# Expert weights of a mixture-of-experts stage laid out by pair of experts and by transfer

## Chip, cores and metric

The kernel runs on one core of one Trainium2 chip. The metric is the device time of one launch in microseconds. Laying out the inputs on the host is not part of it.

## The reference

The reference is two transformer blocks over 256 tokens of 1024 features, in float32. Block 1 is a mixer (gated long convolution, short convolution, pooling), a cross attention and a mixture of 32 experts, of which each token takes 4. Block 2 has attention, retention and feed-forward layers. The change touches the experts only:

```
def clamped_swiglu(gu):
    gate = jnp.minimum(gu[..., :D_EXPERT], SWIGLU_LIMIT)
    up = jnp.clip(gu[..., D_EXPERT:], -SWIGLU_LIMIT, SWIGLU_LIMIT)
    return (up + 1.0) * (gate * jax.nn.sigmoid(gate * SWIGLU_ALPHA))
...
    def step(acc, blk):
        tok, g, e = blk
        xb = h_pad[tok]
        act = clamped_swiglu(xb @ w_gu[e] + b_gu[e])
        yb = act @ w_down[e] + b_down[e]
        return acc.at[tok].add(yb * g[:, None].astype(yb.dtype)), None
```

`w_gu` is 32 x 1024 x 2048 and `w_down` 32 x 1024 x 1024, together 402.7 MB of float32. That is most of the 650.58 MB that the kernel moves.

## The kernel before

Everything is unrolled, on one core. The order on each engine is set by the Tile scheduler, from the order of the code and from a few `issue_after` constraints.

**The experts go in 16 pairs**, numbered 0 to 15 here. A pair's two experts share the array: each has up to 64 token columns (CAP), expert 2i on rows 0 to 63 of the result and expert 2i+1 on rows 64 to 127. For a pair the program does, in order:

- `gather` (L1703): the tokens' rows by one-hot products, done a pair ahead, in two halves;
- `gate_up` (L1716): 8 steps of k, each with 4 banks and 2 experts, every step reading one 2 MB tile `wgu`;
- `swiglu` (L1752 to L1756): the activation, begun by the DVE instruction of L1752 when the first bank of step 7 is done;
- `turn` (L1763, L1764): transposes;
- the down products (L1874): four blocks (j, h), each reading one 2 MB tile `wdn`;
- `combine` (L1770, L1771): the weighted sums go back to the tokens, one pair late.

**The weights** are streamed by SyncE's queue (SP). A pair is 8 tiles `wgu` and 4 tiles `wdn`, 12 x 2 MB = 25.17 MB. Nine buffers of 2 MB take them in turn (five of the pool `raw`, four of a pool `pre`; a tenth is used once). SP issues the transfers in program order, and each waits until the matmuls on the tile nine places earlier are done. The addresses, in `load`:

```
r["g", k] = raw([128, 2, 2 * D], "wgu")
nc.sync.dma_start(r["g", k], A["wgu"][e, 128 * k:128 * k + 128].rearrange("x p n -> p x n"))
...
r["d", j, h] = raw([128, 2, 4, 512], "wdn")
```

In DRAM a row of `wgu` is 8 KB, so a partition's 16 KB of a tile come in two runs of 8 KB, one for each expert. A partition's 16 KB of a `wdn` tile come in eight runs of 2 KB, in two transfers of 1 MB. The other weights (`wpre`, `wpost`, `wadb`; tiles `wraw`, `wadb`) are packed on the host already, and a partition's 16 KB lie together there.

**A branch** (L1855) stands in pair 3: if an expert has more than 64 tokens, `overflow` runs. It is not taken with these inputs. SP waits at the branch until the transfers that it has issued have landed.

After pair 15 come the sums for the norm (`stats`, L1076), the first products of block 2 (`begin`, L399 to L401), and the norm of x3 (L1224 and on).

Of the kernel before, what the change touches and what calls it, by code (L numbers as in the profile page):

```python
# [11 lines left out]
F32 = mybir.dt.float32  # L12
# [51 lines left out]
# ---------------------------------------------------------------- host layout  # L64
# [15 lines left out]
def _slices(w, cols):  # L80
    """[K, 256 columns] -> one [128, 256] slice per 128 rows."""
    b = w[:, cols]
    return [b[k * 128:(k + 1) * 128] for k in range(b.shape[0] // 128)]


def _pack(slices):
    """slices of [128, 256], eight to a block, two blocks to a transfer."""
    n = len(slices)
    while len(slices) % 16:
        slices.append(slices[-1])  # L90
    a = np.stack(slices).reshape(-1, 16, 128, 256)
    return np.ascontiguousarray(a.transpose(0, 2, 1, 3)), n
# [6 lines left out]
def _moba_cols():  # L99
    """columns of a q or k projection: heads 8-15 as chunks of four heads' halves."""  # L100
    idx = list(range(512))
    for g in range(2):
        for half in range(2):
            for h in range(4):
                base = (8 + 4 * g + h) * 64 + half * 32
                idx += list(range(base, base + 32))
    return np.array(idx)


def host_layout(inp):  # L110
# [87 lines left out]
    r["wgu"] = A["w_gu"][0]  # L198
    r["wdn"] = A["w_down"][0]
# [3 lines left out]
    # constants of the shapes alone  # L203
    k = np.arange(128)
    later = -(k[:, None] > k[None, :]).astype(np.float32)       # minus later rows
    earlier = (k[:, None] < k[None, :]).astype(np.float32)      # earlier rows
    io = np.broadcast_to(np.arange(128, dtype=np.float32), (128, 128))
    r["cst4"] = np.ascontiguousarray(np.concatenate([earlier, io], axis=1))
    cst = [np.eye(128, dtype=np.float32)]                       # identity
# [19 lines left out]
    caus = np.where(k[:, None] >= q[None, :], 0.0, NEG)      # [query, key]  # L229
    strict = (k[:, None] < q[None, :])                        # [key, query]  # L230
# [16 lines left out]
# ---------------------------------------------------------------- the program  # L247


class Weights:  # L250
    """A stream of weight slices [128, 256], split into two float32r parts."""
# [23 lines left out]
    def split(self, eng=None):  # L275
        """the next GR slices"""
# [37 lines left out]
def program(ctx: ExitStack, tc: tile.TileContext, A, out, stop=None):  # L314
# [17 lines left out]
    # ---- inputs and constants that stay  # L332
# [53 lines left out]
    class Part:  # L386
        """a product of a block of weights, in parts"""
# [45 lines left out]
    def product_tok(st, XH, XL, kcs, evac, taps=0):  # L433
        """out [128 tokens, 256 features] for both token tiles."""
# [17 lines left out]
    def broad(pool, tag):  # L452
        """two parts of a product's operand with room for columns past the tokens"""
# [23 lines left out]
    def behind(*ins):  # L477
        """what follows queues behind these on their engines"""
# [83 lines left out]
    def normal(src, dst, H, L, c, nm, g, b, func=None):  # L562
        """dst = (src - mean) / deviation * g + b for chunk c, or its two parts"""
# [28 lines left out]
    # ---- modulation vectors of block 2, computed where the array would wait  # L592
# [6 lines left out]
    def silu_c(pool, after=None):  # L599
        """silu of the condition on all partitions"""  # L600
# [7 lines left out]
    def vector_ada(n=1):  # L608
        """modulation vectors by rows, a chunk of 128 to an instruction"""
# [33 lines left out]
    def norm_constants():  # L643
        """weights of the sums which the norm of x3 = (a - mean) / dev * g + b takes from a"""
# [13 lines left out]
    def router_constants():  # L658
        """router weights by gain and a column for the mean; the sums its norm's mean and shift bring"""
# [81 lines left out]
        # ---- pooling windows  # L741
# [23 lines left out]
        # ---- short gated convolution  # L765
# [46 lines left out]
        # ---- memory norm (its own sums, off the main chain)  # L812
# [33 lines left out]
        # ---- keys and values of the memory, spread over the waits of the norms  # L846
# [25 lines left out]
        # ---- norm of the long convolution, and its output  # L872
# [22 lines left out]
        # ---- mix, first norm  # L895
# [24 lines left out]
        # ---- cross attention  # L920
# [76 lines left out]
        # ---- output, and on the way the tokens' rows, their sums and the router's products  # L997
# [56 lines left out]
    # ---- sums over features of the experts' output, tokens on the partitions  # L1054
# [25 lines left out]
    def begin(n):  # L1080
        """the first block of block 2's products, before its input is normalised"""
# [9 lines left out]
    # ======================================================== block 1: experts  # L1091
# [9 lines left out]
    # ======================================================== block 2  # L1101
    wst = post_w
    wst.aside = ASIDE
    with tc.tile_pool(name="wp2", bufs=3, reuse_waits="tile") as wp, tc.tile_pool(name="post", bufs=1, reuse_waits="tile") as post:
# [8 lines left out]
        def project_h(evac, taps=0, into=None):  # L1113
            """a block of the products of the normalised input, the first ones before it is scaled"""
# [110 lines left out]
        # ---- x3 = (a - mean) rs g + b and h = x3 rm gs + shift from sums of a alone  # L1225
# [98 lines left out]
        # ---- layer 0: heads 0-7 by stick-breaking, 8-15 by softmax over their block  # L1324
        with tc.tile_pool(name="att", bufs=1, reuse_waits="tile") as at:
# [123 lines left out]
            def schedule(first, second, half):  # L1449
                """the heads' stages, each a step behind the one before it"""  # L1450
# [33 lines left out]
        # ---- layer 1: retention  # L1484
# [92 lines left out]
def experts(tc, A, B, pre, mo, tmp, psum, X0, consts, Stat, normal, col, eps5, L, x2t, nmu, sd, bgu, es_ins, stats, spread, norm_constants, begin):  # L1577
# [24 lines left out]
    def load(i):  # L1602
# [3 lines left out]
        e = slice(2 * i, 2 * i + 2)  # L1606
        for k in range(NCH):
            r["g", k] = raw([128, 2, 2 * D], "wgu")
            nc.sync.dma_start(r["g", k], A["wgu"][e, 128 * k:128 * k + 128].rearrange("x p n -> p x n"))
        for j in range(2):  # L1610
            for h in range(2):
                r["d", j, h] = raw([128, 2, 4, 512], "wdn")
                if 2 * i + h < 2 * WD or not j:
                    for x in range(2):
                        nc.sync.dma_start(r["d", j, h][:, x], A["wdn"][2 * i + x, 512 * h:512 * h + 512, 512 * j:512 * j + 512].rearrange("(k p) n -> p k n", p=128))
                else:
                    for k in range(4):
                        o = 512 * h + 128 * k
                        nc.sync.dma_start(r["d", j, h][:, :, k], A["wdn"][e, o:o + 128, 512 * j:512 * j + 512].rearrange("x p n -> p x n"))
# [6 lines left out]
    def biased(i, banks, js=range(4)):  # L1626
        """the sums of experts 2i and 2i + 1, begun with their biases"""
# [11 lines left out]
    # ---- router  # L1639
# [25 lines left out]
    # ---- places: how many earlier tokens took the expert  # L1665
# [20 lines left out]
    # ---- one-hot rows, gathering  # L1686
    def gather(i, then=None):
        """the tokens of experts 2i and 2i + 1, CAP columns each; their weighted places"""
# [39 lines left out]
    def residual():  # L1728
        """the norm's output"""
# [46 lines left out]
    def overflow(work):  # L1776
        """Tokens past the first CAP of an expert, any number of them."""
        with tc.For_i(0, NE, 1) as e:
            pc, gc = tmp((128, 2, 1), tag="mx"), tmp((128, 2, 1), tag="sm")
            V.tensor_copy(pc, posm[:, :, bass.ds(e, 1)])  # L1780
            V.tensor_copy(gc, gates[:, :, bass.ds(e, 1)])
            bt = work.tile([4, 512], F32, tag="bo", name="bo")
            nc.sync.dma_start(bt, A["bgu"].rearrange("(e j) n -> e j n", j=4)[bass.ds(e, 1)].rearrange("e j n -> (e j) n"))
            xo = mo.tile([128, D], F32, tag="xs", name="xo")
            act = work.tile([128, D], F32, tag="Y", name="acto")
            at = work.tile([128, D], F32, tag="actT", name="ato")
            actT = at.rearrange("p (k s) -> p k s", k=NCH)

            def piece(src):
                w = tmp((128, 512), tag="pd", bufs=2)  # L1790
                nc.sync.dma_start(w, src.rearrange("e p n -> (e p) n"))
                return w

            for r in range(2):
                pr = tmp((128, 2, 1), tag="mx")
                V.tensor_scalar(pr, pc, float(-(CAP + 128 * r)), None, op0=ALU.add)
                So, Go = tmp((128, 2, 128)), tmp((128, 2, 128))
                for t in range(2):
                    V.tensor_scalar(So[:, t, :], iota, pr[:, t, :], None, op0=ALU.is_equal)
                    V.tensor_scalar(Go[:, t, :], So[:, t, :], gc[:, t, :], None, op0=ALU.mult)  # L1800
                for k in range(NCH):
                    p = psum([128, 128], tag="tp", bufs=2)
                    for t in range(2):
                        PE.matmul(p, x2t[:, t, k * 128:k * 128 + 128], So[:, t, :], start=(t == 0), stop=(t == 1))
                    S.activation(xo[:, k * 128:k * 128 + 128], p, AF.Identity, scale=col("ln2_g", k), bias=col("ln2_b", k))
                gst = psum([128, T], tag="tp", bufs=2)
                for t in range(2):
# [97 lines left out]
```

## Time and profile before

| what | value |
|---|---|
| median of 3 runs | 2246.17 us (2244.93 to 2249.36) |
| span of the profiled execution | 2244.0 us, 2.2 us under that median |
| PE busy | 2103.7 us, 94% |
| DVE, ACT, POOL busy | 54%, 36%, 24% |
| moved by the DMA engines | 650.58 MB, mean 290 GB/s |
| granted clock of TensorE, mean | 0.979 |

Times of the trace count from the span's start. "GB/s" is what the 16 DMA engines moved in a stretch. "DMA share" is the time that their packets took as a share of 16 engines' time; packets overlap a little, so that it can go over 1. The experts' transfers run from about 430 to 1450 us.

### The profile page before, as it was taken

How to read it: one execution, taken by the hardware profiler on the slowest of the kernel's cores; microseconds unless marked ns; L12 is line 12 of the kernel's file. 1: busy time of each engine (PE TensorE's matmuls, PEld its weight loads, DVE VectorE, ACT ScalarE, POOL GpSimd, SP SyncE). 2: the span in 40 equal slices, each digit the busy share in tenths (PEclk: the TensorE clock that was granted, in tenths of full speed). 3: DMA queues.
4: the chain of work that ended last, by engine and by line, in shares of the span. 5: the costliest groups of instructions: out<-in, count | busy, mean ns of one | idle time of the engine just before them, and what ended most of it. 6: DMA issues, size and time to landing. Idle time of an engine off the chain costs nothing.

```text
span 2244.0 us, 33058 instructions
## 1 busy us (share of the span) xinstructions
PE 2103.7 (94%) x13668; PEld 1523.0 (68%) x13668; DVE 1202.3 (54%) x1807; ACT 797.2 (36%) x1374; POOL 544.9 (24%) x452
## 2 busy tenths in 40 slices
PE   8989979999999999999999999889999999999998
PEld 8889978873443333333333333378799999999998
DVE  7999988942222222221112222278788679777554
ACT  5556566641000000000000000157475565556443
POOL 2756396512000000000000000076422124220001
PEclk9999989999999999999999999989999999999999
DMA  8344445589999999999999999954366557555540
GB/s 353 148 155 151 155 186 225 216 338 391 404 414 384 399 408 407 408 409 410 411 411 409 407 408 407 408 195 180 151 260 268 223 195 269 227 224 216 198 151 20
DMA packets 123548, 650.58 MB, mean 290 GB/s; under 512 B 6624, under 2 KB 8544, under 8 KB 76160
## 3 DMA queue, kind: packets, MB, share of 16 engines
q1 hardware_dynamic: 122048, 645.46, 73.1%
q10 hardware_dynamic: 1344, 2.95, 0.4%
q8 instruction: 109, 1.79, 0.3%
q14 instruction: 47, 0.39, 0.0%
HBM read 647.33 MB, written 1.05 MB: 289 GB/s over the span
## 4 chain that ended last, share of the span: by engine, by line
PE 42%; DMA 13%; DVE 8%; ACT 2%; issue 2%; POOL 1%; SPq 1%; DVEq 0%; ACTq 0%; POOLq 0%
DMA wgu<-in_wgu 12%; PE ps_st L1874 9%; PE ps_mm L417 7%; PE ps_mm L419 7%; PE ps_mm L418 7%; PE ps_mm L1716 4%; DVE wl L289 2%; PE ps_tp L1770 2%; DVE act L1756 1%; PE ps_mm L1632 1%; PE ps_tp L1703 1%; POOL tmp_pd L1755 1%; ACT wh L288 1%; DMA wdn<-in_wdn 1%; PE ps_mm L443 1%
## 5 line engine op out<-in xcount | busy, mean ns | idle before, releaser
L289 DVE TENSOR_TENSOR wl<-wraw,wh 128x1024 fp32r<-128x1024 f32 x352 | 500.4, 1426 | 179.7 <-ACT wh L288 175.5
L1716 PE MATMUL ps_mm<-wgu,xs 128*64 128x512 f32 x2048 | 457.2, 595 | 30.9 <-DMA wgu<-in_wgu 30.4
L288 ACT ACTIVATE wh<-wraw 128x1024 fp32r<-128x1024 f32 x356 | 374.4, 1054 | 243.6 <-PE ps_mm L418 218.4
L1716 PEld LDWEIGHTS ps_mm<-wgu,xs 128*64 128x64 f32 x2048 | 144.2, 137 | 315.5 <-issue 256.3
L1752 DVE TENSOR_SCALAR tmp_pd<-ps_mm 128x512 f32<-128x512 f32 x32 | 22.0, 692 | 416.8 <-PE ps_mm L1716 416.8
L1874 PE MATMUL ps_st<-wdn,actT 128*64 128x512 f32 x1024 | 239.9, 597 | 5.7 <-DVE actT L1764 5.6
L417 PE MATMUL ps_mm<-HH,wh 128*128 128x256 f32 x832 | 236.8, 286 | 1.5 <-ACT wh L288 1.2
L419 PE MATMUL ps_mm<-HH,wl 128*128 128x256 f32 x832 | 234.9, 285 | 1.5 <-DVE wl L289 1.5
L418 PE MATMUL ps_mm<-HL,wh 128*128 128x256 f32 x832 | 236.3, 285 | 0.0
L1755 POOL TENSOR_TENSOR tmp_pd<-tmp_pd,tmp_stat 128x512 f32<-128x512 f32 x32 | 40.1, 1275 | 787.5 <-ACT tmp_stat L1753 737.8
L620 POOL TENSOR_TENSOR wadb<-wadb,cb 128x1024 f32<-128x1024 f32 x60 | 169.8, 2855 | 142.0 <-DMA wadb<-in_wadb 86.7
L1753 ACT ACTIVATE tmp_stat<-tmp_pd 128x512 f32<-128x512 f32 x32 | 20.2, 631 | 497.3 <-DVE tmp_pd L1752 497.3
L417 PE MATMUL ps_mm<-pairA,wh 128*128 128x256 f32 x640 | 181.7, 289 | 11.9 <-ACT wh L288 8.5
L419 PE MATMUL ps_mm<-pairA,wl 128*128 128x256 f32 x640 | 181.3, 289 | 4.7 <-DVE wl L289 4.5
L418 PE MATMUL ps_mm<-pairA,wh 128*128 128x256 f32 x640 | 182.5, 287 | 2.3 <-DVE pairA L475 2.3
L1874 PEld LDWEIGHTS ps_st<-wdn,actT 128*64 128x64 f32 x1024 | 75.3, 137 | 142.3 <-issue 132.6
L417 PEld LDWEIGHTS ps_mm<-HH,wh 128*128 128x128 f32 x832 | 159.9, 192 | 2.9 <-ACT wh L288 1.9
L419 PEld LDWEIGHTS ps_mm<-HH,wl 128*128 128x128 f32 x832 | 159.2, 192 | 2.5 <-DVE wl L289 1.9
L418 PEld LDWEIGHTS ps_mm<-HL,wh 128*128 128x128 f32 x832 | 160.1, 192 | 0.8 <-issue 0.7
L417 PEld LDWEIGHTS ps_mm<-pairA,wh 128*128 128x128 f32 x640 | 123.9, 195 | 14.0 <-ACT wh L288 9.1
L419 PEld LDWEIGHTS ps_mm<-pairA,wl 128*128 128x128 f32 x640 | 123.5, 195 | 7.0 <-DVE wl L289 7.0
L418 PEld LDWEIGHTS ps_mm<-pairA,wh 128*128 128x128 f32 x640 | 125.3, 196 | 2.7 <-DVE pairA L475 2.7
(460 smaller groups left out, 4219.1 us busy)
## 6 DMA issues: line engine op xcount, KB each, us to landing
wgu<-in_wgu SPq DMA_DIRECT2D x128, 2048.0 KB, 22.3
wdn<-in_wdn SPq DMA_DIRECT2D x124, 1024.0 KB, 14.5
wraw<-in_wpost SPq DMA_DIRECT2D x56, 2048.0 KB, 8.0
wraw<-in_wpre SPq DMA_DIRECT2D x32, 2048.0 KB, 7.7
wadb<-in_wadb SPq DMA_DIRECT2D x24, 2048.0 KB, 8.9
wdn<-in_wdn SPq DMA_DIRECT2D x8, 512.0 KB, 12.2
wraw<-in_wpre SPq DMA_DIRECT2D x4, 512.0 KB, 7.7
wraw<-in_wpost SPq DMA_DIRECT2D x4, 512.0 KB, 11.8
```

Of the source, the lines that this page charges most:

```text
L288: self.ins = (nc.scalar.activation(wh, src, AF.Copy).ins, (eng or nc.vector).tensor_tensor(wl, src, wh.bitcast(F32), op=ALU.subtract).ins)
L289: (eng or nc.vector).tensor_tensor(wl, src, wh.bitcast(F32), op=ALU.subtract).ins)
L417: PE.matmul(pts[m], wh[:, w], XH[:, kc, :width], start=(i == 0), stop=False)
L418: PE.matmul(pts[m], wh[:, w], XL[:, kc, :width], start=False, stop=False)
L419: PE.matmul(pts[m], wl[:, w], XH[:, kc, :width], start=False, stop=(i == n - 1))
L443: PE.matmul(pts[t], XH[:, kc, x], wl, start=False, stop=False)
L620: G.tensor_tensor(w[:, i, :], w[:, i, :], cbs[0], op=ALU.mult)
L1632: PE.matmul(banks[j][row[x]], ident[:, o:o + 1].to_broadcast([128, CAP]), bgu, start=True, stop=False)
L1716: i_ = PE.matmul(banks[j][row[x]], xs[:, k, row[x]], r["g", k][:, x, 512 * j:512 * j + 512], start=False, stop=(k == NCH - 1))
L1755: G.tensor_tensor(g, g, s, op=ALU.mult)
L1770: PE.matmul(p[:, m, :], Y[:, (2 * c + m) * 128:(2 * c + m) * 128 + 128], GST, start=True, stop=True)
L1874: PE.matmul(yb[j][row[x]], actT[:, k, row[x]], r["d", j, k // 4][:, x, k % 4, :], start=(k == 0), stop=(k == NCH - 1))
```

## The change

Two arrays are laid out on the host in the order of the transfers. `wgu` gets the shape [pair, k, partition, expert, column], and `wdn` [pair, j, h, partition, k, expert, column]. Each 2 MB transfer now reads one block of DRAM in which a partition's 16 KB lie together. A `wdn` tile is one transfer where it was two; the last two tiles of pair 15 are still four transfers of 512 KB each. Inside the tile `wdn` the places of expert and k are exchanged, and the matmuls' slice with them.

`overflow` becomes a loop over pairs with a loop over the two experts inside, since its addresses now need both numbers. Comments are gone too, and line numbers move by one to three.

```diff
-    r["wgu"] = A["w_gu"][0]
-    r["wdn"] = A["w_down"][0]
+    r["wgu"] = np.ascontiguousarray(A["w_gu"][0].reshape(NE // 2, 2, NCH, 128, 2 * D).transpose(0, 2, 3, 1, 4))
+    r["wdn"] = np.ascontiguousarray(A["w_down"][0].reshape(NE // 2, 2, 2, 4, 128, 2, 512).transpose(0, 5, 2, 4, 3, 1, 6))
...
-        e = slice(2 * i, 2 * i + 2)
         for k in range(NCH):
             r["g", k] = raw([128, 2, 2 * D], "wgu")
-            nc.sync.dma_start(r["g", k], A["wgu"][e, 128 * k:128 * k + 128].rearrange("x p n -> p x n"))
+            nc.sync.dma_start(r["g", k], A["wgu"][i, k])
         for j in range(2):
             for h in range(2):
-                r["d", j, h] = raw([128, 2, 4, 512], "wdn")
+                r["d", j, h] = raw([128, 4, 2, 512], "wdn")
                 if 2 * i + h < 2 * WD or not j:
-                    for x in range(2):
-                        nc.sync.dma_start(r["d", j, h][:, x], A["wdn"][2 * i + x, 512 * h:512 * h + 512, 512 * j:512 * j + 512].rearrange("(k p) n -> p k n", p=128))
+                    nc.sync.dma_start(r["d", j, h], A["wdn"][i, j, h])
                 else:
                     for k in range(4):
-                        o = 512 * h + 128 * k
-                        nc.sync.dma_start(r["d", j, h][:, :, k], A["wdn"][e, o:o + 128, 512 * j:512 * j + 512].rearrange("x p n -> p x n"))
+                        nc.sync.dma_start(r["d", j, h][:, k], A["wdn"][i, j, h, :, k])
...
-        with tc.For_i(0, NE, 1) as e:
+        with tc.For_i(0, NE // 2, 1) as e:
+            with tc.For_i(0, 2, 1) as x:
+                overflow_of(work, e, x)
...
-                    PE.matmul(yb[j][row[x]], actT[:, k, row[x]], r["d", j, k // 4][:, x, k % 4, :], start=(k == 0), stop=(k == NCH - 1))
+                    PE.matmul(yb[j][row[x]], actT[:, k, row[x]], r["d", j, k // 4][:, k % 4, x, :], start=(k == 0), stop=(k == NCH - 1))
```

The scheduler also orders a few instructions differently. On SP, the end of pair 5's transfers and the start of pair 6's, before:

```order
320 L1609 DMA wgu_7261<-in_wgu 128x2x2048
321 L1615 DMA wdn_7263<-in_wdn 128x4x512 x2
322 L1615 DMA wdn_7266<-in_wdn 128x4x512 x2
323 L1615 DMA wdn_7269<-in_wdn 128x4x512 x2
324 L1615 DMA wdn_7272<-in_wdn 128x4x512 x2
325 L1609 DMA wgu_7474<-in_wgu 128x2x2048
```

The same place in the changed kernel:

```order
325 L1609 DMA wgu_7253<-in_wgu 128x4096
326 L1614 DMA wdn_7255<-in_wdn 128x4096
327 L1614 DMA wdn_7257<-in_wdn 128x4096
328 L1614 DMA wdn_7259<-in_wdn 128x4096
329 L1614 DMA wdn_7261<-in_wdn 128x4096
330 L1609 DMA wgu_7462<-in_wgu 128x4096
```

The tiles come in the same order, and 12 transfers stand where 16 stood.

On PE, where pair 4's `combine` meets the first step of pair 5 (`ps_tp` from `Y` is `combine`, `ps_tp` from `z` is `gather`, `ps_mm` is `gate_up`), before:

```order
3640 L1770 MATMUL ps_tp_7376<-tmp_t_7193,Y_7210 128x256 x2
3641 L1770 MATMUL ps_tp_7380<-tmp_t_7193,Y_7210 128x256 x2
3642 L1703 MATMUL ps_tp_7391<-tmp_t_7384,z_5056 128x128 x8
3643 L1716 MATMUL ps_mm_7275<-wgu_7247,xs_7163 64x512 x2
3644 L1716 MATMUL ps_mm_7278<-wgu_7247,xs_7163 64x512 x2
3645 L1716 MATMUL ps_mm_7281<-wgu_7247,xs_7163 64x512 x2
3646 L1716 MATMUL ps_mm_7284<-wgu_7247,xs_7163 64x512 x2
3647 L1703 MATMUL ps_tp_7404<-tmp_t_7384,z_5056 128x128 x8
3648 L1716 MATMUL ps_mm_7275<-wgu_7249,xs_7163 64x512 x2
```

The same place in the changed kernel:

```order
3647 L1768 MATMUL ps_tp_7364<-tmp_t_7185,Y_7202 128x256 x2
3648 L1768 MATMUL ps_tp_7368<-tmp_t_7185,Y_7202 128x256 x2
3649 L1714 MATMUL ps_mm_7263<-wgu_7239,xs_7155 64x512 x2
3650 L1714 MATMUL ps_mm_7266<-wgu_7239,xs_7155 64x512 x2
3651 L1714 MATMUL ps_mm_7269<-wgu_7239,xs_7155 64x512 x2
3652 L1714 MATMUL ps_mm_7272<-wgu_7239,xs_7155 64x512 x2
3653 L1701 MATMUL ps_tp_7379<-tmp_t_7372,z_5056 128x128 x8
3654 L1701 MATMUL ps_tp_7392<-tmp_t_7372,z_5056 128x128 x8
3655 L1714 MATMUL ps_mm_7263<-wgu_7241,xs_7155 64x512 x2
```

Both halves of `gather` now stand behind step 0; before, step 0 stood between them.

On ACT, in the norm after the experts (`wh` is a part of block 2's weights, `tmp_t` from `tmp_r4` serves the norm's broadcast), before:

```order
657 L1244 ACTIVATE tmp_u_9890<-tmp_u_9890,kc_93 128x2
658 L288 ACTIVATE wh_10102<-wraw_10048 128x1024
659 L491 ACTIVATE tmp_t_9977<-cst_69,tmp_r4_9885 128x128
660 L491 ACTIVATE tmp_t_9980<-cst_69,tmp_r4_9885 128x128
661 L1253 ACTIVATE tmp_mu_9907<-ps_tp_9908 128x256
```

The same place in the changed kernel:

```order
663 L1245 ACTIVATE tmp_u_9840<-tmp_u_9840,kc_93 128x2
664 L492 ACTIVATE tmp_t_9927<-cst_69,tmp_r4_9835 128x128
665 L492 ACTIVATE tmp_t_9930<-cst_69,tmp_r4_9835 128x128
666 L289 ACTIVATE wh_10052<-wraw_9998 128x1024
667 L1254 ACTIVATE tmp_mu_9857<-ps_tp_9858 128x256
```

The weights' part `wh` moved behind the two `tmp_t`.

## Rows read from the trace of the kernel before

**Rows 1.** The page: the span in 40 equal slices.

```profile
PE   8989979999999999999999999889999999999998
DMA  8344445589999999999999999954366557555540
```

**Rows 2.** The page: DMA packets, and issues (count, KB each, us to landing).

```profile
DMA packets 123548, 650.58 MB, mean 290 GB/s; under 512 B 6624, under 2 KB 8544, under 8 KB 76160
...
wgu<-in_wgu SPq DMA_DIRECT2D x128, 2048.0 KB, 22.3
wdn<-in_wdn SPq DMA_DIRECT2D x124, 1024.0 KB, 14.5
```

**Rows 3.** The chain, pairs 5 to 15: start, us, what (L1752 begins a pair's activation).

```profile
821.18 0.70 DVE tmp_pd L1752
...
878.65 0.70 DVE tmp_pd L1752
...
936.12 0.70 DVE tmp_pd L1752
...
1022.71 33.81 DMA wgu<-in_wgu
...
1057.68 0.70 DVE tmp_pd L1752
...
1119.25 0.70 DVE tmp_pd L1752
...
1428.18 0.70 DVE tmp_pd L1752
```

**Rows 4.** Stretches: busy us of each engine (x), clock, DMA share, GB/s.

```profile
12.00:40.00 28.00, 27.58 (x226) 27.17 (x226) 21.55 (x30) 14.97 (x23) 6.72 (x7) 1.00 1.02 429
1022.00:1056.00 34.00, 30.74 (x154) 12.85 (x152) 1.80 (x3) 0.38 (x1) 0.00 (x0) 1.00 1.01 418
1057.00:1077.00 20.00, 19.11 (x88) 6.78 (x86) 9.44 (x17) 3.37 (x7) 3.27 (x4) 1.00 1.05 390
...
960.00:1430.00 470.00, 429.64 (x2008) 164.64 (x2006) 87.26 (x156) 27.98 (x63) 22.43 (x27) 1.00 1.02 409
...
560.00:720.00 160.00, 153.59 (x732) 67.34 (x729) 40.90 (x74) 11.37 (x24) 9.79 (x12) 0.99 1.02 407
...
728.70:809.10 80.40, 78.63 (x382) 33.28 (x380) 15.00 (x26) 4.11 (x9) 3.26 (x4) 1.00 1.00 401
...
240.00:260.00 20.00, 19.04 (x156) 18.43 (x155) 17.69 (x31) 10.14 (x15) 7.27 (x7) 1.00 0.56 211
```

**Rows 5.** PE around `gather` and step 0: start, us, line, tiles, count.

```profile
849.38 2.05 PE L1703 MATMUL ps_tp<-tmp_t,z 128*128 128x128 f32 x16
851.36 3.65 PE L1716 MATMUL ps_mm<-wgu,xs 128*64 128x512 f32 x16
```

**Rows 6.** Waits, 960 to 1430 us: total us, times, longest.

```profile
PE ps_mm L1716 <- DMA wgu<-in_wgu: 30.4, 27, 1.4
```

**Rows 7.** SP, the last `wgu` of pair 5: issue, and us to landing; PE's end of step 7.

```profile
L1609 SPq DMA_DIRECT2D wgu<-in_wgu x1: 367/367/367, 784.9 to 784.9; - x1
...
DMA to landing us min/median/max: 24.2/24.2/24.2
...
823.53 1.03 PE L1632 MATMUL ps_mm<-moec,cst 128*64 128x512 f32 x4
```

**Rows 8.** SP at the branch, and its last transfer before it.

```profile
L1855 SPq EVENT_SEMAPHORE  x8: 17/17/17, 723.1 to 728.5; - x8
...
L1609 SPq DMA_DIRECT2D wgu<-in_wgu x1: 368/368/368, 700.0 to 700.0; - x1
...
DMA to landing us min/median/max: 28.1/28.1/28.1
```

**Rows 9.** ACT in the norm after the experts.

```profile
1473.74 1.06 ACT L288 ACTIVATE wh<-wraw 128x1024 fp32r<-128x1024 f32 x1 [3.21 <-PE ps_mm L418]
1474.70 0.68 ACT L491 ACTIVATE tmp_t<-cst,tmp_r 128x128 f32<-128x128 f32 x2
```

More of the change, by code (lines that the diff above doesn't have):

```diff
@@ L1776, in overflow @@
     def overflow(work):
-        with tc.For_i(0, NE, 1) as e:
[L1779 to L1797, printed above, removed]
-                for t in range(2):
[L1799 to L1807, printed above, removed]
-                    PE.transpose(gst[:, t * 128:t * 128 + 128], Go[:, t, :], ident)
-                GST = tmp()
-                V.tensor_copy(GST, gst)
-                banks = [psum([128, 512]) for _ in range(4)]
-                for j in range(4):
-                    PE.matmul(banks[j], ident[0:4, j:j + 1].to_broadcast([4, 128]), bt, start=True, stop=False)
-                for k in range(NCH):
-                    for j in range(4):
-                        w = piece(A["wgu"][bass.ds(e, 1), k * 128:k * 128 + 128, 512 * j:512 * j + 512])
-                        PE.matmul(banks[j], xo[:, k * 128:k * 128 + 128], w, start=False, stop=(k == NCH - 1))
-                swiglu(banks, act)
-                turn(act, actT)
-                yb = [psum([128, 512], tag="st", bufs=2) for _ in range(2)]
-                for k in range(NCH):
-                    for j in range(2):
-                        w = piece(A["wdn"][bass.ds(e, 1), k * 128:k * 128 + 128, 512 * j:512 * j + 512])
-                        PE.matmul(yb[j], actT[:, k, :], w, start=(k == 0), stop=(k == NCH - 1))
-                for j in range(2):
-                    V.tensor_copy(act[:, 512 * j:512 * j + 512], yb[j])
-                combine(act, GST)
@@ new lines, in overflow, with overflow_of, piece @@
+        with tc.For_i(0, NE // 2, 1) as e:
+            with tc.For_i(0, 2, 1) as x:
+                overflow_of(work, e, x)
+    def overflow_of(work, e, x):
+        pc, gc = tmp((128, 2, 1), tag="mx"), tmp((128, 2, 1), tag="sm")
+        V.tensor_copy(pc, posm[:, :, bass.ds(2 * e + x, 1)])
+        V.tensor_copy(gc, gates[:, :, bass.ds(2 * e + x, 1)])
+        bt = work.tile([4, 512], F32, tag="bo", name="bo")
+        nc.sync.dma_start(bt, A["bgu"].rearrange("(e j) n -> e j n", j=4)[bass.ds(2 * e + x, 1)].rearrange("e j n -> (e j) n"))
+        xo = mo.tile([128, D], F32, tag="xs", name="xo")
+        act = work.tile([128, D], F32, tag="Y", name="acto")
+        at = work.tile([128, D], F32, tag="actT", name="ato")
+        actT = at.rearrange("p (k s) -> p k s", k=NCH)
+        def piece(src):
+            w = tmp((128, 512), tag="pd", bufs=2)
+            nc.sync.dma_start(w, src.rearrange("e p x n -> (e p) (x n)"))
+            return w
+        for r in range(2):
+            pr = tmp((128, 2, 1), tag="mx")
+            V.tensor_scalar(pr, pc, float(-(CAP + 128 * r)), None, op0=ALU.add)
+            So, Go = tmp((128, 2, 128)), tmp((128, 2, 128))
+            for t in range(2):
+                V.tensor_scalar(So[:, t, :], iota, pr[:, t, :], None, op0=ALU.is_equal)
+                V.tensor_scalar(Go[:, t, :], So[:, t, :], gc[:, t, :], None, op0=ALU.mult)
+            for k in range(NCH):
+                p = psum([128, 128], tag="tp", bufs=2)
+                for t in range(2):
+                    PE.matmul(p, x2t[:, t, k * 128:k * 128 + 128], So[:, t, :], start=(t == 0), stop=(t == 1))
+                S.activation(xo[:, k * 128:k * 128 + 128], p, AF.Identity, scale=col("ln2_g", k), bias=col("ln2_b", k))
+            gst = psum([128, T], tag="tp", bufs=2)
+            for t in range(2):
+                PE.transpose(gst[:, t * 128:t * 128 + 128], Go[:, t, :], ident)
+            GST = tmp()
+            V.tensor_copy(GST, gst)
+            banks = [psum([128, 512]) for _ in range(4)]
+            for j in range(4):
+                PE.matmul(banks[j], ident[0:4, j:j + 1].to_broadcast([4, 128]), bt, start=True, stop=False)
+            for k in range(NCH):
+                for j in range(4):
+                    w = piece(A["wgu"][bass.ds(e, 1), k, :, bass.ds(x, 1), 512 * j:512 * j + 512])
+                    PE.matmul(banks[j], xo[:, k * 128:k * 128 + 128], w, start=False, stop=(k == NCH - 1))
+            swiglu(banks, act)
+            turn(act, actT)
+            yb = [psum([128, 512], tag="st", bufs=2) for _ in range(2)]
+            for k in range(NCH):
+                for j in range(2):
+                    w = piece(A["wdn"][bass.ds(e, 1), j, k // 4, :, k % 4, bass.ds(x, 1), :])
+                    PE.matmul(yb[j], actT[:, k, :], w, start=(k == 0), stop=(k == NCH - 1))
+            for j in range(2):
+                V.tensor_copy(act[:, 512 * j:512 * j + 512], yb[j])
+            combine(act, GST)
```

## The prediction

> **What bounds the kernel now.** I read the page's slices first, then the DMA part, the chain through the experts, stretches chosen from that chain, and the waits. The page's slices [rows 1] show two kernels in one: before and after the experts, DMA is a third to two thirds busy and PE is full; through the experts (slices 9 to 25) DMA stands at 9 tenths, and PE is nearly full as well. So in this stage the two are close, and the question is which ends last, pair by pair.
>
> The chain answers it [rows 3]. The activation's first instruction (L1752) marks one moment of each pair. From pair 5 to 6 it takes 57.47 us (821.18 to 878.65), from 6 to 7 57.47 again (936.12), and between them the chain holds no transfer: that is the pace of the PE program. From pair 9 to 10 it takes 61.57 (1057.68 to 1119.25), and each pair has a piece like the 33.81 us of DMA at 1022.71: there the weights set the pace. The check: 25.17 MB over the 409 GB/s of that stretch [rows 4] is 61.5 us. The waits agree: PE stands 30.4 us in 27 gaps for a `wgu` [rows 6]. So only the time from about pair 7 on is bound by DMA; earlier pairs lived on a lead. How large the lead was: the last `wgu` of pair 5 landed at 784.9 + 24.2 = 809.1, and its step begins 16 matmuls before the row at 823.53 [rows 7]; a step takes 3.44 us (the row at 851.36, 3.65 for 16 matmuls, less the last one's tail of 0.2 [rows 5]). That is 820.1, a lead of 11.0 us. At 61.5 - 57.47 = 4.1 us lost per pair it lasts 2.7 pairs, to somewhere in pair 8, and the marks from there on are the slow ones.
>
> **What the change does to the transfers.** It removes no byte. It makes runs of 16 KB out of 8 KB (`wgu`) and 2 KB (`wdn`). The trace has all three kinds in streams that fill the DMA engines [rows 4]: `wgu` alone (1022 to 1056) 418 GB/s at share 1.01; `wdn` alone (1057 to 1077) 390 at 1.05; packed weights of 16 KB (12 to 40) 429 at 1.02. The check on the first two: 16.78 MB at 418 and 8.39 at 390 are 40.1 + 21.5 = 61.6 us, the measured pair. I take 429 for the new transfers: they have the same shape, size and queue as the `wraw` of that stretch, and PE, DVE and ACT were busier there. A pair then needs 25.17 / 0.429 = 58.66 us, still 1.2 over the 57.47 of PE.
>
> **Whether the lead now lasts.** Ten pairs follow pair 5. Nine cost 58.66 - 57.47 = 1.19 of lead each. The last step is shorter for PE, since pair 15 gathers for nobody: two halves of 1.98 us (851.36 - 849.38) [rows 5] fall away, 57.47 - 3.96 = 53.51, and costs 5.15. Together 15.9 us. The lead at pair 5 grows: the 80.4 us from the branch to 809.1 ran at 401 GB/s [rows 4], at 429 they save 80.4 x (1 - 401/429) = 5.2, so 16.2. Besides, SP left the branch at 728.5, right after its last transfer landed at 700.0 + 28.1 = 728.1 [rows 8]: this is a drain of a full queue. The stretch before it, 160 us at 407, would save up to 8.2, and SP resumes that much sooner. PE does not wait for it, but the lead becomes up to 24. Against 15.9 both ends suffice; the experts go at PE's pace to the end.
>
> **The sum.** From pair 7's mark to pair 15's took 1428.18 - 936.12 = 492.06 us. At PE's pace it is 7 x 57.47 + 53.51 = 455.80. The difference is 36.3 us. A second reading gives the same size: the 30.4 us of gaps count from the modelled end of a matmul, 0.2 later than the pace, and 27 x 0.2 makes 35.8.
>
> What else moves:
> - 62 issues fewer on SP (two `wdn` transfers become one): zero, since SP's issue is ahead of the data (24.2 us from issue to landing in rows 7); uncovered, nothing on the path issues there.
> - `gather` behind step 0 on PE: the same 1.98 + 1.98 us of work in another place; PE passes both without a gap now [rows 5] and its products are needed a pair later. Zero; if each pair stood 0.5 us for a buffer, 11 x 0.5 = 5.5 more.
> - ACT's `wh` behind two `tmp_t` in the norm: `wh` waits 3.21 us for PE and holds up the two [rows 9]. They are now free of that wait. If the chain goes through them it saves up to 3.2; if through `wh`, which still waits for PE, it costs up to 0.7. I take zero.
> - The nested loop of `overflow`: not run; its branches stand behind a branch that is not taken. Zero.
> - What is late next: PE itself, in the experts too. Block 2 starts 36 us sooner and is unchanged.
>
> The span 2244.0 becomes 2207.7; the median lies 2.2 above the span, so I expect 2246.2 - 36.3 = 2209.9 us. The rest, 3.2 down and 5.5 up, is the likeliest case's own range: 2206 to 2216.
>
> **The rivals.**
>
> *The 16 KB rate falls short.* The stretch at 429 is short (28 us). A straight line through the other two kinds gives less: a 2 KB packet takes 16 x 2048 / 390 = 84.0 ns of an engine, an 8 KB packet 16 x 8192 / 418 = 313.6, so 0.0374 ns a byte and 7.5 ns a packet; a 16 KB packet 619.8, or 423 GB/s. A pair is then 59.5 us, the ten steps cost 9 x 2.03 + 5.99 = 24.3, and the lead is 11 + 4.2 to 11 + 10.2. PE stands 3 to 9 us at the end: a gain of 27 to 33, time 2213 to 2219. The point from which it decides is some 427 GB/s with the small lead. Against it: 429 was measured, not drawn.
>
> *The length of a run doesn't matter*, and 390 against 418 comes from something else that the layout keeps (the place in the kernel, the buffers written). Then the stage stays at 409 and the time at 2246. Against it: `wdn` and `wgu` go to the same buffers on the same queue, alternate every 20 to 40 us, and differ in their runs.
> The Trainium skill ("DMA: Bandwidth & Descriptors", Specifications) would side with this rival: it puts the least run for line rate at 512 B, and all runs here are longer. By that rule the sum is zero; the two rates of rows 4 speak against it.
>
> *8 KB runs are as good as 16.* If only `wdn` gained and both kinds went at 418, a pair would be 25.17 / 0.418 = 60.2 us; ten steps cost 9 x 2.73 + 6.7 = 31.3 against a lead of 14 to 19; the gain is 19 to 24, time 2222 to 2227.
> The Trainium skill (the same page, Why small descriptors are slow (HBM only)) gives 3 fixed cycles per packet beside 32 B per cycle: as an estimate from it, 2 KB runs lose 4.7%, 8 KB runs 1.2% and 16 KB runs 0.6%, a pair would take 60.5 us, and the time would be near 2230. The rows show a larger difference between 2 and 8 KB, 7%.
>
> *The other sign: the stage gets slower.* One block of 2 MB for each transfer changes where in DRAM the 16 engines read at one time. Where packed weights run alone they show 211 GB/s at share 0.56 (240 to 260) [rows 4], 377 per full share, under the 409 of now. If the new transfers went at 377, a pair would take 66.8 us, the lead of 11 would be gone in little over a pair, and pair 15's last `wgu`, now just ahead of the mark at 1428.18 [rows 3], would land near 809 + 5 + 10 x 66.8 = 1482: 55 us later, time near 2301. It decides below 409. Against it: 211 at 0.56 is a stream with pauses, and the same kind without pauses made 429.
>
> **How the numbers follow.** PE's pace to the end, 2206 to 2216: 0.70. Short rate, up to 2219: 0.11. 8 KB as good as 16, up to 2227: 0.06. More than this (the norm's order saves 3 or more as well): 0.06. No difference: 0.04. Slower: 0.03. The range 2204 to 2221 leaves out some 2 in 10 at most. A change of 0.2% is 4.5 us, about what a measurement of this kernel can tell from none; every case but the last two is faster by more: 0.93, 0.04, 0.03.
>
> **What the profile after would show.** Packets fall from 123,548 by 72,960 (98,304 runs of 2 and 8 KB become 24,320 of 16 KB and 1,024 of 4 KB) to about 50,600, with some 11,600 under 8 KB where 76,160 were [rows 2]; `wgu` and `wdn` in issues of 2048 KB, 128 and 62. The stretch of the experts shows 425 to 435 GB/s while DMA is full. The marks of L1752 stand 57.5 us apart from pair 5 to pair 14, and 53.5 at the last; no DMA piece of 33 us is on the chain; PE's waits for `wgu` go from 30.4 us to under 3. SP leaves the branch at 720 to 725. The prediction is wrong if marks at the end are 59 us or more apart (the rate), if the pace of PE itself isn't 57.5 (the order), or if block 2, from pair 15's mark to the end 815.8 us now, takes another time.

## The result and the profile after

The changed kernel takes 2213.12 us (median of 4 runs, 2211.63 to 2213.84), the kernel before 2247.77 beside it (2244.93 to 2250.79): a ratio of 0.9849, interval 0.983 to 0.9867. Timed again later, beside other kernels, it gave 2214.66 and 0.9862 (0.9837 to 0.9887). The forecast was 2209.9, with a range of 2204 to 2221. The profiled execution has a span of 2211.4 us, 32.6 under that of before.

The page of the changed kernel: slices of PE and DMA, packets, and the issues of `wdn` (count, KB each, us to landing); those of `wgu` are 128 of 2048 KB, as before. They answer to [rows 1, 2].

```profile
PE   8999979999999999999999999879999999999998
...
DMA  8344455589999999999999999943377566555540
...
DMA packets 49596, 650.57 MB, mean 294 GB/s; under 512 B 5632, under 2 KB 7552, under 8 KB 10656
...
wdn<-in_wdn SPq DMA_DIRECT2D x62, 2048.0 KB, 20.2
```

The bytes are the same and the packets fewer by 73,952, which is 992 more than the runs explain. The packets under 512 B fell by just 992, 16 for each of the 62 issues that are gone.

Stretches of the changed kernel, against [rows 4]: the packed weights of 16 KB, a piece from the branch on, the experts, and their last pairs (columns as in [rows 4]).

```profile
12.00:40.00 28.00, 27.51 (x227) 27.11 (x227) 22.18 (x31) 15.76 (x24) 7.09 (x7) 1.00 1.01 427
...
720.00:810.00 90.00, 88.03 (x428) 36.92 (x426) 15.53 (x27) 4.52 (x10) 3.26 (x4) 1.00 0.97 408
900.00:1000.00 100.00, 96.45 (x474) 38.86 (x472) 22.04 (x39) 7.07 (x15) 6.53 (x8) 1.00 1.01 427
...
1300.00:1390.00 90.00, 84.23 (x396) 31.42 (x392) 14.31 (x27) 4.65 (x13) 2.50 (x2) 1.00 1.01 427
```

The experts' weights now come at the 427 GB/s of the packed weights, where 409 stood. Only the piece from the branch on, which begins with an empty queue, shows less: 408. The chain of the changed kernel answers to [rows 3]; L1750 is what L1752 was, the first instruction of a pair's activation, and the rows are the marks of pairs 5, 6, 7 and of 13, 14, 15.

```profile
819.38 0.70 DVE tmp_pd L1750
...
876.44 0.70 DVE tmp_pd L1750
...
933.50 0.70 DVE tmp_pd L1750
...
1276.13 0.70 DVE tmp_pd L1750
...
1297.10 35.27 DMA wgu<-in_wgu
...
1333.54 0.70 DVE tmp_pd L1750
...
1352.62 38.55 DMA wgu<-in_wgu
...
1392.34 0.70 DVE tmp_pd L1750
```

A step is the distance of one mark from the next. It takes 57.06 us, and the eight steps from pair 5 to 13 are all within 0.3 of that (456.75 for eight). Then a piece of DMA comes back twice: the last two steps take 57.41 and 58.80. The wait that was 30.4 us in 27 gaps [rows 6] is down to four gaps (total, times, longest):

```profile
PE ps_mm L1714 <- DMA wgu<-in_wgu: 5.0, 4, 1.2
```

Laid beside the marks of before, the 32.6 us of span come from three places: 1.8 up to pair 5's mark, 34.0 between the marks of pairs 5 and 15 (607.0 before, 572.96 now), and a loss of 3.2 from pair 15's mark to the end (815.8 before, 819.1 now).

### The profile page after: what moved, and what is told of

Read it like the earlier page. It is cut to its first block, busy times and chain, and to the rows that moved or that the text cites. A ratio compares the mean times of both kernels' runs of the same rounds, so it can differ in the third digit from the quotient of the medians.

```text
span 2211.4 us, 32998 instructions
## 1 busy us (share of the span) xinstructions
PE 2091.1 (95%) x13668; PEld 1518.2 (69%) x13668; DVE 1206.3 (55%) x1807; ACT 796.9 (36%) x1374; POOL 540.1 (24%) x452
## 2 busy tenths in 40 slices
DMA packets 49596, 650.57 MB, mean 294 GB/s; under 512 B 5632, under 2 KB 7552, under 8 KB 10656
## 4 chain that ended last, share of the span: by engine, by line
PE 49%; DVE 8%; issue 4%; DMA 3%; ACT 3%; POOL 1%; DVEq 0%; ACTq 0%; POOLq 0%
PE ps_mm L1714 10%; PE ps_st L1877 7%; PE ps_mm L420 7%; PE ps_mm L418 7%; PE ps_mm L419 7%; DMA wgu<-in_wgu 3%; PE ps_tp L1768 2%; DVE wl L290 2%; PE ps_tp L1701 2%; DVE act L1754 1%; POOL tmp_pd L1753 1%; PE ps_mm L444 1%; PE ps_mm L443 1%; PE ps_mm L445 1%; ACT wh L289 1%
## 5 line engine op out<-in xcount | busy, mean ns | idle before, releaser
L1877 PE MATMUL ps_st<-wdn,actT 128*64 128x512 f32 x1024 | 230.6, 597 | 5.7 <-DVE actT L1762 5.6
L1750 DVE TENSOR_SCALAR tmp_pd<-ps_mm 128x512 f32<-128x512 f32 x32 | 22.1, 692 | 379.7 <-PE ps_mm L1714 379.7
```

Of the source, the lines that this page charges most:

```text
L1877: PE.matmul(yb[j][row[x]], actT[:, k, row[x]], r["d", j, k // 4][:, k % 4, x, :], start=(k == 0), stop=(k == NCH - 1))
```

## Experiments

The theory was that the length of a run in DRAM sets the rate, and that this rate decides the stage. The rivals were the number of issues, the connected block of 2 MB, and a rate that is full already at some shorter run. Twelve kernels ran. "Bound steps" below are distances of marks once the lead is gone.

| kernel | us | ratio to before | bound steps |
|---|---|---|---|
| gate/up alone (`wgu_only`) | 2239.05 | 0.9977 (0.9961 to 0.9993) | 60.83 |
| down alone (`wdn_only`) | 2222.94 | 0.9905 (0.9882 to 0.9928) | 59.39 |
| down in blocks, 2 KB runs (`wdn_2k_block`) | 2240.76 | 0.9970 (0.9952 to 0.9987) | 60.82 |
| both in blocks, 8 KB (`runs_8k`) | 2229.11 | 0.9927 (0.9905 to 0.9949) | 59.7 |
| both in blocks, 4 KB (`runs_4k`) | 2249.40 | 1.0007 (0.9993 to 1.0020) | 61.4 |
| 16 KB, partitions far apart (`pitch_16k`) | 2234.27 | 0.9934 (0.9912 to 0.9957) | 60.0 to 61.1 |
| new layout, old order (`xk_two`) | 2219.84 | 0.9872 (0.9852 to 0.9891) | 59.19 |
| half of down (`half_wdn`) | 2199.65 | 0.9778 (0.9755 to 0.9802) | none |
| half of down from pair 12 on (`half_wdn_late`) | 2206.32 | 0.9813 (0.9791 to 0.9834) | none |
| branch in pair 14 (`branch_14`) | 2216.21 | 0.9861 (0.9837 to 0.9885) | 58.8 to 59.1 |
| branch in pair 1 (`branch_1`) | 2219.62 | 0.9874 (0.9851 to 0.9898) | 59.1 to 60.0 |
| the changed kernel again (`changed_again`) | 2214.66 | 0.9862 (0.9837 to 0.9887) | 58.4 |

**One half of the change at a time.** The first kernel keeps the old `wdn`, the second the old `wgu`. Here and below, `...` stands for the addresses and slices that go with the new shape:

```diff
-    r["wdn"] = np.ascontiguousarray(A["w_down"][0].reshape(NE // 2, 2, 2, 4, 128, 2, 512).transpose(0, 5, 2, 4, 3, 1, 6))
+    r["wdn"] = A["w_down"][0]
...
```
```diff
-    r["wgu"] = np.ascontiguousarray(A["w_gu"][0].reshape(NE // 2, 2, NCH, 128, 2 * D).transpose(0, 2, 3, 1, 4))
+    r["wgu"] = A["w_gu"][0]
...
```

> Only the gate/up weights are laid out anew; the down weights keep the old layout (two issues a tile, runs of 2 KB). Theory (the length of the run sets the rate): a pair costs 8 x 4.90 + 4 x 5.40 = 60.8 us of transfers, 0.6 less than before, so over the ten bound steps some 6 to 8 us come off: about 2240 (2236 to 2243). Rival (only the 2 KB runs were slow, 8 KB as good as 16): no gain, 2246 to 2249. Rival (both layouts gave the same share): half of the 34.6 us, about 2230.

> Only the down weights are laid out anew; the gate/up weights keep runs of 8 KB. Theory (length of the run): a pair costs 8 x 4.98 + 4 x 4.90 = 59.4 us and some 0.3 of gaps, 1.8 less than before, and the lead grows by 4 to 8: 2219 to 2228. Rival (8 KB as good as 16, the gain was all in the 2 KB runs): as the whole change, 2211 to 2216. Rival (both layouts gave the same share): about 2230.

Measured: 2239.05 and 2222.94, both inside the theory's ranges and outside those of the two rivals. The bound steps, 60.83 and 59.39, are the sums of the transfers written down ahead (60.8 and 59.4). Most of the gain is in `wdn`, whose runs were shortest, and the rest in `wgu`.

**The same blocks, other runs.** Three kernels keep one issue and one connected block of 2 MB for each transfer, and change how the block is cut. Here `wdn` in runs of 2 KB; the other two cut both kinds, into 4 KB and into 8 KB, in the same way:

```diff
-    r["wdn"] = np.ascontiguousarray(A["w_down"][0].reshape(NE // 2, 2, 2, 4, 128, 2, 512).transpose(0, 5, 2, 4, 3, 1, 6))
+    r["wdn"] = np.ascontiguousarray(A["w_down"][0].reshape(NE // 2, 2, 2, 4, 128, 2, 512).transpose(0, 5, 2, 3, 1, 4, 6))
...
-                    nc.sync.dma_start(r["d", j, h], A["wdn"][i, j, h])
+                    nc.sync.dma_start(r["d", j, h], A["wdn"][i, j, h].rearrange("k x p n -> p k x n"))
...
```

> As the changed kernel, with one issue and one connected block of 2 MB for each transfer of down weights, but in rows of 2 KB inside the block (8 runs to a partition). Theory (length of the run): these transfers stay at 5.4 us for 2 MB, and the time is that of the run with the gate/up weights alone, 2236 to 2243. Rival (one issue in place of two, or one connected block, made the gain): 2211 to 2216.

> As the changed kernel, one connected block of 2 MB and one issue for every transfer, but in runs of 8 KB (two to a partition), for both kinds of weights. Theory (length of the run): 12 x 4.98 = 59.8 us a pair and 0.3 of gaps, 1.0 more than the changed kernel, over ten steps 8 to 12 us more: 2221 to 2227. Rival (block or issue count): 2211 to 2216.

> The changed kernel with connected blocks of 2 MB in runs of 4 KB, both kinds of weights. Theory (a fixed price for each packet: 84.4, 311 and 612 ns for 2, 8 and 16 KB lie on 9 ns + 0.0368 ns a byte): 160 ns for 4 KB, 5.11 us for 2 MB, 61.3 us a pair and some gaps, so steps of 61.3 to 61.6 once the lead is gone, about as before: 2244 to 2253. Rival (from 4 KB on the rate is full, only 2 KB is short): as the run with 8 KB, 2226 to 2233, or better.

The 2 KB kernel is as slow as the one that keeps the old `wdn`, to 0.01 us in the bound steps: neither the single issue nor the block made the gain. A stretch of its last pairs, at 413 GB/s where `wgu_only` has 412:

```profile
1300.00:1390.00 90.00, 83.68 (x396) 32.47 (x394) 21.88 (x38) 6.11 (x14) 4.50 (x6) 1.00 1.03 413
```

A stretch of 100 us in the experts of `runs_8k`:

```profile
1200.00:1300.00 100.00, 91.46 (x446) 35.68 (x444) 20.14 (x36) 6.74 (x14) 6.54 (x8) 1.00 1.01 421
```

and of `runs_4k`:

```profile
1200.00:1300.00 100.00, 90.51 (x438) 35.77 (x434) 14.40 (x25) 4.13 (x9) 3.26 (x4) 1.00 1.03 409
```

With the 390 of [rows 4] for 2 KB and the 427 above for 16 KB, an engine's packet takes 84.0, 160.2, 311.3 and 613.9 ns (16 x bytes / rate). The last two give a straight line of 8.7 ns a packet and 0.0369 ns a byte; it puts 4 KB at 160.0 and 2 KB at 84.4, within 0.4 ns of what stands there. (Rates in whole GB/s leave the 8.7 uncertain by some 1.5.) In these blocks a fixed price for each packet accounts for the whole difference. The time of `runs_4k` was forecast from such a line (2244 to 2253) and came to 2249.4. `runs_8k` came 2 us above its range. In its profile pair 0's mark stood 3.6 us later than in the changed kernel (525.8), and the step from pair 1 to 2 took 72.0 us for 69.35, with a mean granted clock of 0.97 from 560 to 690 (1.00 in the changed kernel).

By the Trainium skill ("DMA: Bandwidth & Descriptors", Specifications) every run of 512 B or more is at line rate. The 390, 409, 421 and 427 GB/s for 2, 4, 8 and 16 KB disagree. The Trainium skill (the same page, Why small descriptors are slow (HBM only)) gives some 3 fixed cycles a packet beside one for each 32 B: as an estimate from it, a fixed part worth 96 B. The form agrees; the size doesn't, for the measured 8.7 ns are worth 8.7 / 0.0369 = 236 B.

**The same runs, far apart.** The partition becomes the outermost index in DRAM:

```diff
-    r["wgu"] = np.ascontiguousarray(A["w_gu"][0].reshape(NE // 2, 2, NCH, 128, 2 * D).transpose(0, 2, 3, 1, 4))
-    r["wdn"] = np.ascontiguousarray(A["w_down"][0].reshape(NE // 2, 2, 2, 4, 128, 2, 512).transpose(0, 5, 2, 4, 3, 1, 6))
+    r["wgu"] = np.ascontiguousarray(A["w_gu"][0].reshape(NE // 2, 2, NCH, 128, 2 * D).transpose(3, 0, 2, 1, 4))
+    r["wdn"] = np.ascontiguousarray(A["w_down"][0].reshape(NE // 2, 2, 2, 4, 128, 2, 512).transpose(4, 0, 5, 2, 3, 1, 6))
...
```

> The changed kernel with the partition as the outermost index in DRAM: each run is still 16 KB, but the 128 runs of a transfer lie 2 MB (gate/up) or 1 MB (down) apart in place of next to each other. Theory (the length of the run alone): 2211 to 2217, 4.90 us for 2 MB. Rival (the connected block of 2 MB has a part in the gain): slower transfers, 5.0 us and more, 2220 or above.

The rival won: 2234.27. Packets (49,596) and the instructions of the engines are those of the changed kernel, and the stretch of the experts shows it:

```profile
1200.00:1300.00 100.00, 91.14 (x446) 35.53 (x442) 20.15 (x36) 6.73 (x14) 6.52 (x8) 1.00 1.01 417
```

Most transfers land 4.9 us after the one before, as in the changed kernel, but from 900 us on a quarter of them 5.1 or more. So "the length of a run alone" fell as a theory. Where the 128 runs lie matters too; here it costs 417 against 427. In the old layout it cost nothing for `wdn`, since blocks with runs of 2 KB were no faster than its rows. The distances here are powers of two; no run has another distance, so that it stays open which of the two matters.

The Trainium skill ("DMA: Bandwidth & Descriptors", Latency and other measured facts) has a row for copies of 16 KB runs from HBM to HBM, with 164 GB/s a direction at a pitch of 2 MB where the full rate is 214. The direction agrees, the size doesn't: these loads keep 417 of 427.

**Are the last two steps weights?** Two kernels load only half of each `wdn` tile, for all pairs or from pair 12 on:

```diff
-                    nc.sync.dma_start(r["d", j, h], A["wdn"][i, j, h])
+                    nc.sync.dma_start(r["d", j, h][:, 0:2], A["wdn"][i, j, h, :, 0:2])
...
-                    PE.matmul(yb[j][row[x]], actT[:, k, row[x]], r["d", j, k // 4][:, k % 4, x, :], start=(k == 0), stop=(k == NCH - 1))
+                    PE.matmul(yb[j][row[x]], actT[:, k, row[x]], r["d", j, k // 4][:, k % 2, x, :], start=(k == 0), stop=(k == NCH - 1))
```

> The changed kernel that loads only half of each tile of down weights (1 MB of 2 MB, runs of 8 KB; the products read the loaded half twice, so that the output is another). A pair then needs 8 x 4.90 + 4 x 2.45 = 49 us of transfers, far under PE's 57.06. Theory (the last two steps of the changed kernel, 57.4 and 58.8, are weights again): the steps become 57.06 and 57.06 - 3.84 (no gather) = 53.2, 6 us less: 2205 to 2209. Rival (PE's own program is slow there): both steps stay, 2211 to 2215.

> As the run with half of the down weights, but halved for pairs 12 to 15 alone (output is another); up to pair 11 all is as in the changed kernel. Theory (the last two steps of the changed kernel wait for weights): marks equal to the changed kernel's up to pair 11, then steps of 56.6 to 57.1 and a last one of 52 to 53.3; pair 15's mark at about 1385 in place of 1392. Rival: steps of 57.4 and 58.8 at the end as before, mark at 1392.

The scheduler wove `gather` and `combine` otherwise in both, so `half_wdn` is no clean comparison over its whole length: it gains 15 us between the marks of pairs 5 and 15, and loses 10 after them. Its 2199.65 is below the theory's 2205 to 2209; its mark of pair 5 already stands 5.8 us sooner. `half_wdn_late` has the changed kernel's instructions up to pair 11, and its steps of 57.06. Its marks stand some 2.9 us later from pair 5 on, so that pair 15's is at 1387.4 and not at the 1385 expected. Its last marks in the chain are those of pairs 12 to 15:

```profile
1221.95 0.70 DVE tmp_pd L1750
...
1278.58 0.70 DVE tmp_pd L1750
...
1335.22 0.70 DVE tmp_pd L1750
...
1387.40 0.70 DVE tmp_pd L1750
```

Steps of 56.64 and a last one of 52.18, without a wait for weights. So the 57.41 and 58.80 of the changed kernel are weights, and PE alone would take 57.06 - (56.64 - 52.18) = 52.6 for the last step: 0.35 + 6.2 = 6.5 us are lost there.

**The branch.** SP's last transfer before the branch landed 23.5 us after its issue at 698.6, at 722.1; SP then issued at 722.7, and the next landing was at 730.4, 8.3 us later where 4.9 is the rule. Two kernels move the branch out of pair 3:

```diff
-        if i == 3:
+        if i == 14:
             load(i + 1)
```

> The changed kernel with the branch on the overflow moved from pair 3 to pair 14, behind the last loads of weights. Theory (SP empties its queue at the branch, which cost the stream of weights 3.4 us: 8.3 between two landings in place of 4.9; and PE, which stands 4.0 there, has slack in pair 14): the last weights land 3.4 us sooner, the marks from about pair 12 on go at 59: 2208 to 2211. Rival (the stop on PE in pair 14 comes on top, since the weights land sooner than it needs them): 2213 to 2217.

> The same with the branch in pair 1, where SP stands for buffers anyway. Theory: the emptied queue falls together with a stop that is there already (16 us without an issue from 521 and again from 577), the weights land up to 3.4 sooner at the end and PE pays the same stop: 2209 to 2212. Rival (nothing is saved, since the stream has to stop once anyway): 2213.

Neither gains: `branch_14` came out as its rival said, `branch_1` above both of its forecasts. In `branch_14` the marks up to pair 14 are earlier, 1330.1 in place of 1333.5, but SP stood at the branch with the last three `wgu` not issued (the scheduler had put them behind it). The first of them then took 7.8 us to land on an empty queue, as the first after the branch in pair 3 does, and the last landed at 1391.3, as in the changed kernel (1391.2). PE's stop came on top: 63.8 us for the last step. In `branch_1` the step from pair 1 to 2 became 82.8 us where it was 69.35; PE alone stood 5.0 at the branch.

**Order against layout.** The instructions of PE and ACT stand otherwise in the changed kernel (`gather` whole behind step 0). `wgu_only` has the order of before; the others so far, but for the half loads and the moved branches, have that of the changed kernel. `xk_two` puts the expert ahead of the row in the `wdn` tile and loads it in two issues, which gives the old order with the new layout:

```diff
-    r["wdn"] = np.ascontiguousarray(A["w_down"][0].reshape(NE // 2, 2, 2, 4, 128, 2, 512).transpose(0, 5, 2, 4, 3, 1, 6))
+    r["wdn"] = np.ascontiguousarray(A["w_down"][0].reshape(NE // 2, 2, 2, 4, 128, 2, 512).transpose(0, 5, 2, 4, 1, 3, 6))
...
-                    nc.sync.dma_start(r["d", j, h], A["wdn"][i, j, h])
+                    [nc.sync.dma_start(r["d", j, h][:, x], A["wdn"][i, j, h, :, x]) for x in range(2)]
...
```

> New layout, old order: a tile of down weights lies as [partition, expert, 4 rows, 512] and is loaded in two issues of 1 MB, one for each expert, with runs of 8 KB; gate/up weights in runs of 16 KB. The instructions of PE, ACT, DVE and POOL then stand in the order of the kernel before. A pair needs 8 x 4.90 + 4 x 4.98 = 59.1 us of transfers and some gaps. Theory (the order, not the layout, sets PE's pace of 57.06 and the 3 to 6 us lost after the experts): steps of 57.47 until the lead is gone, then 59.1 to 59.4; pair 15's mark about 3 us later than in the changed kernel, and 814 to 816 us from it to the end: 2209 to 2213. Rival (the loss after the experts comes with the layout): 818 to 822 to the end, 2214 to 2219.

Half of the theory held. Where no weights are waited for, steps take 57.47 us in the three kernels with the old order (before, `wgu_only`, `xk_two`) and 57.06 in the ones with the new: PE's pace goes with the order. The three also load a `wdn` tile in two issues, and no run parts the two; but the chain finds the difference where the order differs (below). From pair 15's mark to the end `xk_two` takes 821.6 us, so the loss after the experts does not belong to the order, and the time, 2219.84, is just above the rival's. It does not belong to the layout alone either. The largest single piece of it is a stretch at a lower granted clock (the third figure from the end of a row: 0.50 is 1.2 GHz, 1.00 is 2.4 GHz), here in the changed kernel,

```profile
1543.10:1560.20 17.10, 17.10 (x68) 12.59 (x66) 7.08 (x31) 6.20 (x20) 7.46 (x10) 0.50 0.08 35
```

here in the same kernel in its second profile,

```profile
1548.00:1561.70 13.70, 13.70 (x57) 10.24 (x57) 6.12 (x26) 5.32 (x16) 5.50 (x8) 0.50 0.00 1
```

and here in the kernel before:

```profile
1589.30:1592.70 3.40, 3.40 (x22) 3.17 (x21) 2.95 (x10) 2.14 (x4) 1.28 (x2) 0.50 0.00 0
```

> The changed kernel as it is, timed beside the three others. Near 2213. In its profile the question is the stretch after the experts: if the 17 us at half clock (1543 to 1560 in the first profile) belong to the layout, they come again at the same place; if they are chance, the half-clock stretches stand elsewhere.

The stretch at half clock came again, 155 us after pair 15's mark. With 13.7 or 17.1 us it begins at 151 to 160 in eight of the fourteen profiles. `half_wdn` has 10.2 at 167, the kernel before 3.4 at 161; `wgu_only`, `runs_8k`, `branch_1` and `half_wdn_late` have none there. Over it the changed kernel falls back by some 6 us against the kernel before (from 3 ahead, counted from the mark, to 3 behind). `branch_1` and `runs_8k`, which have the new layout and no such stretch, need 817.7 and 818.4 to the end; the two kernels with the old `wdn` need 815.8 and 814.0. The place is not the whole of it: `half_wdn_late` has none there but 17.1 us at half clock 70 us behind the mark, and needs 820.1. What decides whether and where such a stretch comes is open.

No kernel here that loads all its weights beats the changed one by more than the interval.

## Why the prediction was right, and where it was not

The direction, the range and the mechanism held. Step by step:

- **The rate.** Forecast 429, measured 427; the packed weights, 429 before, stand at 427 in this profile too. The transfers of a pair are 12 x 4.90 = 58.8 us (58.66 forecast); the last step, bound by them, took 58.80. The two half changes and the three cuts of the block show run by run that this is the cause.
- **The lead.** The last `wgu` of pair 5 was issued at 783.3 and landed 17.0 later; its step began at 818.3 (16 matmuls ahead of the L1630 row at 821.74). That is a lead of 18.0, inside the 16 to 24. Its parts were otherwise: from the branch to that landing it took 77.6 us where 80.4 stood, 2.8 saved and not 5.2 (408 GB/s from 720 to 810, not 429). That stretch began 6.0 us sooner (722.7 for 728.7), and PE's step 1.8: 11.0 + 2.8 + 6.0 - 1.8 = 18.0.
- **"Against 15.9 both ends suffice; the experts go at PE's pace to the end"** is the step that failed. The small end of the lead was only 0.3 over the 15.9, and two terms of these were mis-sized. The ten pairs from 800.3 to the landing of pair 15's last `wgu` at 1391.2 took 59.09 us each, not 58.66, since some landings come later than 4.9 after the one before. And PE needs 57.06, not 57.47, for a pair, and 52.6, not 53.5, for the last. The loss over ten steps is 590.9 - (9 x 57.06 + 52.6) = 24.8. Less the lead of 18.0 that leaves 6.8 us, and the marks show the same: 572.96 - 566.14 = 6.8. The last two steps hold 6.5 of it, and `half_wdn_late` shows that these go with the weights; the other 0.3 is the step from pair 8 to 9, as long there.
- **The sum.** From pair 7's mark to pair 15's the gain was 492.06 - 458.84 = 33.2 where 36.3 was forecast. These 6.8 were lost, and PE's faster program gave back 7 x 0.41 + 0.9 = 3.8.
- **`gather` behind step 0: zero, at most 5.5 more** had the wrong sign, and left out a second place. PE gains 0.41 us a pair. The chain shows 9.35 from `combine`'s last piece to step 1 where it was 9.53: 0.18 is `gather`'s. The other 0.24 stands in the down products, 17.47 from their first matmul to that piece where it was 17.71: `combine`'s first piece comes behind 32 of them now, behind 34 before. The orders listed under the change do not have that exchange.
- **ACT's order in the norm: zero, at most 3.2 saved** was 0.8 saved: from DVE's first part of block 2's weights (`wl`) after pair 15's mark to its fourth it takes 31.6 us in both profiles of the changed kernel and 32.4 in `xk_two`, which has the old order.
- **SP** left the branch at 722.7, in the 720 to 725 forecast. Issues cost nothing that a run shows: one issue in place of two left `wdn_2k_block` at the pace of `wgu_only`.
- **"Block 2 is unchanged"** failed: 819.1 us and not 815.8. The instructions are the same but for the few that changed places; the clock granted to them was not, and what decides that is open.

So the forecast of 2207.7 for the span missed by 3.7: 2.2 between the marks of pairs 5 and 15 (36.3 forecast, 34.0 measured; pairs 5 to 7 gained 0.8) and 3.2 after them, against 1.8 gained ahead of pair 5. That the miss is so small is in part luck: 6.8 lost at the end of the experts and 3.2 in block 2 stand against 3.8, 0.8 and 1.8 of gains that were not forecast either.

Of the signs that the prediction gave for being wrong two came: PE's pace is 57.06 and not 57.5, and block 2 takes another time. The third did not, since the marks at the end are 58.80 apart at most. The last step of 53.5, the waits under 3 us (5.0) and a chain without a long piece of DMA (35.27 and 38.55) failed with the lead. The packets came to 49,596 for some 50,600.

Of the rivals, the short rate of 423 GB/s did not come, but its picture did: PE stands some us at the end, and the time lies at the edge of its 2213 to 2219. "The length doesn't matter" and "8 KB as good as 16" fell with `wdn_only` and `runs_8k`. The slower side was not met, though `pitch_16k` shows that the place of the runs in DRAM can take more than half of the gain (14 us are left of 34).

## What to carry to other kernels

When transfers bound a stage, fit the price of a packet over run lengths that stand in a full stream: 8.7 ns and 0.0369 ns a byte give the usual bound step of every connected layout here within 0.2 us. A fit of the two short lengths alone, from the kernel before, gave 423 GB/s for 16 KB where 427 came; a measured stretch of the new length, 429, was nearer. Then compare the sum of transfers for one round of the loop with the compute of that round, and add up the lead to the very last round: here transfers of 59.09 us against PE's 57.06 showed only in the ninth of ten rounds. A change that makes one side faster also moves the other (here PE's order), so the lead has to be recounted with both new paces.

## What the runs showed of the hardware

- The price of a run from 2 to 16 KB is linear here: 84.0, 160.2, 311.3 and 613.9 ns of an engine for 2, 4, 8 and 16 KB. Each issue brings 16 more packets under 512 B (992 for 62).
- An issue of 2 MB takes SP 0.33 us in 16 KB runs. In a full stream of 4 KB runs it holds SP for about as long as the data take (a median of 4.88 us, where 2 MB land every 5.1), as this row of `runs_4k` shows (SP's issues, ns min/median/max):

```profile
L1609 SPq DMA_DIRECT2D wgu<-in_wgu x12: 908/4876/10407, 1120.4 to 1198.6; - x12
```

- At the branch SP waits until all that it issued has landed [rows 8], and the stream shows a hole wherever the branch stands: 8.3 us between two landings in pair 3, 8.1 in pair 14, where 4.9 is the rule.
- PE was busy in all of the 17.1 us at half clock and nearly so in the stretch ahead of it, as this row of the changed kernel shows; what makes the clock fall there is open.

```profile
1520.00:1543.00 23.00, 22.68 (x172) 19.37 (x171) 18.09 (x40) 15.64 (x37) 10.45 (x13) 1.00 0.19 66
```
